# Output projection by seven block products instead of eight, in two rounds of 1024 channels

## The chip, the cores and the metric

One core of one Trainium2 chip runs the kernel. The metric is the device time of one launch in microseconds (us). The kernel before takes 2109.77 us, the median of 2 runs (2109.26 and 2110.27).

## The reference, cut to what matters

The block normalises x (2048 tokens by 1024), projects it by `w_in` to 7168 channels, and makes two branches of 1024 channels: a gated long convolution (Hyena, `y_a`) and a spatial gating unit (gMLP, `y_b`). The change touches the last two lines alone:

```python
y = jnp.concatenate([y_a, y_b], axis=-1) @ w_out      # (2048, 2048) @ (2048, 1024)
x = x + rms_norm(y, post_norm_w)
```

All of it is float32. The kernel reaches that accuracy by splitting each operand into a rounded high part and a remainder (`hi` and `lo`, type float32r) and summing three matmuls, hi·hi + lo·hi + hi·lo (`mm3`, L273 to L277).

## The kernel before, in words

**The input projection** is a stream of 56 pairs of 128-channel blocks (`stream`, L616). A pair is a 2 x 2 block product done with seven block products in place of eight (Winograd's form of Strassen's scheme). The weights are the stationary operand, in seven units of 128 x 512 that are read from DRAM, combined (`comb`, L545) and split (`prep_unit`, L556). The tokens are the moving operand, seven tiles `x0` to `x6` that stay in SBUF for 28 pairs; for the second half of the tokens they are summed early, kept in DRAM (`XS`) and read back by `load_x` (L509), which splits them again. One product is 4 k-steps of 3 matmuls of 512 columns, so a pair is 7 x 12 = 84 matmuls. Products 5 and 6 of a pair come after product 0 of the next one. The classes `TakeU`, `TakeG`, `TakeB`, `TakeV` add the partial sums from PSUM and pass them on.

**Stages.** Beside the stream, `tick` (every second step of the stream) advances background jobs and starts new ones at a given rate. The stages in their order, each with its own SBUF pool: filter MLP and its transform (`k1_jobs`); `x_jobs`, which make `XS`; `kfft_jobs`, ending with the switch to the second half of the tokens; pool `fb`, the **u stage**: pairs U(1), whose `u_job` and `u1_job` convolve, gate, transpose and transform u; pool `fc`: pairs G, V and B with `fft_jobs` and the inverse transform; then the output projection. In pool `fb` there are 4 tiles of 128 x 1024 (tag `wide`: `r1`, `rv`, `t1`, `t2` of a pair) and 3 of 128 x 512 (tag `f`: `uh`, `ul`).

**The output projection.** During the last pair, `load_wo` (L1046) reads `w_out` (8 MB) in 16 pieces through `wide` tiles, splits them, and keeps all of it in the place of `x0` to `x6`. `first_out` (L1092) does token blocks 0 and 1 at once, `out_phase` (L1100) the other 14: for a block, 2 halves x 16 channel blocks x 3 = 96 matmuls of 512 columns; then square and sum (L1144), times `post_norm_w` (L1149), reciprocal root, scale and residual (L1153), store (L1154). For 16 blocks that is 1536 matmuls.

**Order.** The order on each engine and queue is made by a planner when the program is built. It goes by estimated times: when an engine is free it issues, of the instructions that are ready by the plan, the one that stands first in the program; a tile gets its buffer at that moment. On the chip every engine and DMA queue then keeps that order and waits by semaphore. Most DMAs are issued by SyncE (SP).

Of the kernel before, what the change touches and what calls it, by code (L numbers as in the profile page):

```python
# [215 lines left out]

class Body:
# [77 lines left out]
    def build(self):  # L295
        with ExitStack() as st:
# [12 lines left out]
            self.Y = dram("Y", [NJ, 128, 16, 128])  # L309
            self.RB = dram("RB", [D])  # L310
# [4 lines left out]
            self.yq = {}  # L315
# [5 lines left out]
            self.order = B(0) + U(0) + GV(0) + U(1) + GV(1) + B(1)  # L321
# [4 lines left out]
            with self.pool("rp") as self.rp:  # L326
# [33 lines left out]
            with self.pool("op") as op:  # L360
                self.out_phase(op)
# [147 lines left out]
    def load_x(self, u):  # L509
# [3 lines left out]
        nc.sync.dma_start(t[:, 1].bitcast(F32), self.XS[u])  # L513
# [15 lines left out]
    def prep_begin(self, n):  # L529
# [5 lines left out]
        again = (kind, c) in self.seen  # L535
        self.seen.add((kind, c))
        w = [self.i["w_in"][b].rearrange("p (h k) c -> p h (k c)", h=2) for b in (b1, b2)]
# [18 lines left out]
    def prep_unit(self, rec):  # L556
# [17 lines left out]
        if u in SPILL and not again:  # L574
# [12 lines left out]
    def product(self, x, w, u, ps, first=True, last=True):  # L587
        po = ps.rearrange("q (i t) -> q i t", i=4)
        for k in range(4):
            c = slice(k * 128, k * 128 + 128)  # L590
            self.mm3(po, w[u][:, 0, c], w[u][:, 1, c], x[u][:, 0, :, c], x[u][:, 1, :, c],
                     first and k == 0, k == 3, skip_group_check=True)

    def finish_pair(self, new):
# [3 lines left out]
        x, w, take, B, C, u2 = self.prev  # L598
        self.prev = None
        self.product(x, w, 5, B, first=False)  # L600
# [3 lines left out]
        self.product(x, w, 6, C, first=False)  # L604
# [4 lines left out]
    def reload(self, new, u):  # L609

        if new == "wo":
            self.load_wo(u)
        elif new is not None:
            self.load_x(u)

    def stream(self, pairs, new=None):  # L616

        for n in range(pairs):
            h, kind, c, b1, b2 = self.order[self.at]
            take = {"U": TakeU, "G": TakeG, "B": TakeB, "V": TakeV}[kind](self, h, c)  # L620
            key, _, _, w = self.next_w
            x, rec = dict(self.X), self.next_w
            change = new if n == pairs - 1 else None
            while not w:
                self.prep_unit(rec)
            B = self.bank("proj")
            self.product(x, w, 0, B)
# [5 lines left out]
            self.next_w = self.prep_begin(self.at)  # L633
# [3 lines left out]
            self.product(x, w, 1, A)  # L637
# [4 lines left out]
            self.product(x, w, 2, B, first=False)  # L642
# [5 lines left out]
            self.product(x, w, 3, C)  # L648
# [3 lines left out]
            self.product(x, w, 4, B, first=False)  # L652
# [5 lines left out]
            self.prev = (x, w, take, B, C, u2)  # L658
# [387 lines left out]
    def load_wo(self, u):  # L1046


        if u == 0:
            self.xh, self.xl = [], []  # L1050
        if u % 2 == 0:
            self.xh.append(self.xp.tile([128, 4, D], F32R, name=f"wo{u}", tag=f"x{u}"))
            if u < 6:
                return
            lo = [self.wp.tile([128, D], F32R, name="wol", tag="wu", bufs=5) for _ in range(4)]
        else:
            t = self.xp.tile([128, 4, D], F32R, name=f"wo{u}", tag=f"x{u}")
            lo = [t[:, q] for q in range(4)]
        self.xl.append(lo)
        nc, n = self.nc, u // 2  # L1060
        for q in range(4):
            c = 4 * n + q
            raw = self.wide([128, D], "wo_raw")
            nc.sync.dma_start(raw, self.i["w_out"][c * 128:(c + 1) * 128])
            nc.scalar.copy(self.xh[n][:, q], raw)
            nc.vector.tensor_tensor(lo[q], raw, self.xh[n][:, q].bitcast(F32), op=ALU.subtract)

    def out_mms(self, ps, h, r, hi, lo):

        sl = slice(h * 512, h * 512 + 512)  # L1070
        for q in range(4):
            self.mm3(ps, hi[:, q], lo[:, q], self.xh[r][:, q, sl], self.xl[r][q][:, sl], r == 0 and q == 0, r == 3 and q == 3)

    def first_tokens(self, j):

        parts = []
        for s in range(2):
            raw = self.two("yraw")
            self.nc.sync.dma_start(raw.rearrange("q s (c p) -> q (s c) p", c=4), self.Y[j, :, 8 * s:8 * s + 8])
            if j == 0 and s:  # L1080
                pair = [[self.f("yq", F32R) for _ in range(2)] for _ in range(2)]
            else:
                tag, bufs = ("wide", self.nw_) if j else ("two", self.nl)
                pair = [[t[:, 0], t[:, 1]] for t in [self.fp.tile([128, 2, 512], F32R, name="yq", tag=tag, bufs=bufs) for _ in range(2)]]
            for r in range(2):
                hi, lo = pair[0][r], pair[1][r]
                self.nc.scalar.copy(hi, raw[:, r])
                self.nc.vector.tensor_tensor(lo, raw[:, r], hi.bitcast(F32), op=ALU.subtract)
                parts.append([x.rearrange("q (c p) -> q c p", c=4) for x in (hi, lo)])
        return parts  # L1090

    def first_out(self):  # L1092
        self.banks = {}
        for j in range(2):
            parts = self.first_tokens(j)
            self.banks[j] = [self.bank("proj" if j == 0 else "b") for _ in range(2)]
            for h, r in [(h, r) for h in range(2) for r in range(3)] + [(0, 3), (1, 3)]:
                self.out_mms(self.banks[j][h], h, r, *parts[r])

    def out_phase(self, op):  # L1100
        nc, i = self.nc, self.i
        xv = i["x"].rearrange("(p j) d -> j p d", j=NJ)
        ov = self.out.rearrange("(p j) d -> j p d", j=NJ)
        pw = op.tile([128, D], F32, name="pw")
        nc.scalar.dma_start(pw, i["post_norm_w"].partition_broadcast(128))
        jk = op.tile([128, 512], F32, name="jk")
        z = lambda: op.tile([128, 512], F32, name="z", bufs=4)
        xt = lambda j: op.tile([128, D], F32, name=f"xt{j % 2}")
        q = lambda j: op.tile([128, 8, 128], F32R, name=f"q{j % 2}", bufs=4)
        ld = lambda: op.tile([128, 8, 128], F32, name="yraw", bufs=4)  # L1110

        first = {"z": [z()], 0: [xt(0)], 3: [q(3)], 1: [xt(1)], 2: [q(2)], "ld": [ld()]}
# [74 lines left out]
```

## Time and profile before

| | |
|---|---|
| median of 2 runs | 2109.77 us |
| the profiled execution | 2112.95 us, span 2111.2 us |
| TensorE matmul busy | 1944.8 us (92%), 8024 matmuls, mean granted clock 0.974 |
| TensorE weight load busy | 1451.6 us (69%) |
| VectorE (DVE) busy | 1217.0 us (58%) |
| ScalarE (ACT) busy | 786.5 us (37%) |
| GpSimd (POOL) busy | 378.8 us (18%) |
| DMA moved | 469.75 MB, mean 223 GB/s |

Times are microseconds from the start of the span unless marked ns. A matmul's busy time (0.39 us) is longer than its share of the engine, because matmuls are pipelined; where they follow each other without a gap, the time of a stretch divided by their number counts. An engine's idle time is put down to what released it last. The rows themselves are in the section after the change.

### The profile page before, as it was taken

The page shows a single profiled execution, that of the slowest core. Times are in us where ns is not written, and L with a number is a line of the kernel's source. Part 1 is how long each engine was busy: PE and PEld are TensorE (multiplying, and loading weights), DVE is VectorE, ACT ScalarE, POOL GpSimd, SP SyncE. Part 2 cuts the span into 40 slices and gives each one's busy share as a digit, 9 for nine tenths or more (in the row PEclk, how much of TensorE's full clock was granted, in tenths as well). Part 3 has the DMA queues.
Part 4 walks back from the last instruction along what each step waited for, and adds up shares of the span by engine and source line. Part 5 has one row for each costly group of instructions (what it writes and reads, how often), then busy time and mean ns, then how long its engine had stood idle before and what let it go on. Part 6 is the DMA issues. An engine that isn't in the chain of part 4 may idle for free.

```text
span 2111.2 us, 23743 instructions
## 1 busy us (share of the span) xinstructions
PE 1944.8 (92%) x8024; PEld 1451.6 (69%) x8024; DVE 1217.0 (58%) x1912; ACT 786.5 (37%) x1426; POOL 378.8 (18%) x342
## 2 busy tenths in 40 slices
PE   3698999998999989899999999899999996999998
PEld 3465666777776766677776566557677775788887
DVE  6768877787564645744446889778642243322221
ACT  5344444664544434444543232233222232211110
POOL 3421322223222111111111101001011100100100
PEclk9899999999999999999999999999999998999999
DMA  5388776785879778866668878797989864432311
GB/s 143 108 265 279 231 260 235 245 287 204 270 241 303 256 276 260 295 174 200 204 203 257 289 255 278 257 289 254 298 271 291 273 216 159 160 110 90 107 63 40
DMA packets 318105, 469.75 MB, mean 223 GB/s; under 512 B 106363, under 2 KB 176251, under 8 KB 317055
## 3 DMA queue, kind: packets, MB, share of 16 engines
q1 hardware_dynamic: 251232, 393.44, 57.5%
q10 hardware_dynamic: 61856, 69.81, 9.8%
q0 software_dynamic: 4896, 4.98, 1.0%
q8 instruction: 64, 1.05, 0.2%
q14 instruction: 57, 0.47, 0.1%
HBM read 286.74 MB, written 181.41 MB: 222 GB/s over the span
## 4 chain that ended last, share of the span: by engine, by line
PE 47%; DVE 7%; DMA 4%; issue 2%; ACT 1%; POOL 0%; SPq 0%; DVEq 0%; ACTq 0%; POOLq 0%
PE proj L277 11%; PE proj L276 11%; PE proj L275 11%; PE b L1035 3%; PE b L1009 2%; PE b L997 2%; DVE pb L1000 1%; DMA wo_raw<-in_w_out_dram 1%; PE b L275 1%; DVE pa L1000 1%; PE b L276 1%; PE b L277 1%; PE b L924 1%; DVE t L807 1%; DVE pa L1004 1%
## 5 line engine op out<-in xcount | busy, mean ns | idle before, releaser
L275 PE MATMUL proj<-x,wu 128*128 128x512 f32 x1568 | 658.0, 420 | 24.6 <-ACT x L461 13.1
L276 PE MATMUL proj<-x,wu 128*128 128x512 f32 x1568 | 632.9, 404 | 8.7 <-DVE wu L570 6.9
L277 PE MATMUL proj<-x,wu 128*128 128x512 f32 x1568 | 632.1, 403 | 0.6 <-POOL x L462 0.6
L275 PEld LDWEIGHTS proj<-x,wu 128*128 128x128 f32 x1568 | 299.0, 191 | 113.5 <-issue 29.5
L570 POOL TENSOR_TENSOR wu<-wraw,wu 128x512 fp32r<-128x512 f32 x140 | 207.6, 1484 | 929.5 <-ACT wu L568 747.7
L276 PEld LDWEIGHTS proj<-x,wu 128*128 128x128 f32 x1568 | 299.0, 191 | 94.4 <-issue 25.4
L277 PEld LDWEIGHTS proj<-x,wu 128*128 128x128 f32 x1568 | 298.9, 191 | 76.0 <-issue 13.0
L568 ACT CAST wu<-wraw 128x512 fp32r<-128x512 f32 x168 | 104.0, 619 | 250.5 <-PE proj L277 214.0
L275 PE MATMUL proj<-wo,q 128*128 128x512 f32 x448 | 174.3, 389 | 0.9 <-ACT q L1122 0.9
L276 PE MATMUL proj<-wo,q 128*128 128x512 f32 x448 | 174.4, 389 | 0.5 <-DVE q L1123 0.5
L570 DVE TENSOR_TENSOR wu<-ws,wu 128x512 fp32r<-128x512 f32 x112 | 83.7, 748 | 101.4 <-ACT wu L568 101.3
L581 ACT COPY sn<-proj 128x512 f32<-128x512 f32 x168 | 97.7, 582 | 90.5 <-PE proj L277 75.2
L277 PE MATMUL proj<-wo,q 128*128 128x512 f32 x336 | 130.7, 389 | 0.0
L568 ACT CAST wu<-ws 128x512 fp32r<-128x512 f32 x112 | 69.2, 619 | 116.9 <-PE proj L277 89.8
L1000 DVE TENSOR_TENSOR pa<-b,k 64x512 f32<-64x512 f32 x128 | 87.4, 683 | 41.9 <-PE b L997 28.3
L275 PEld LDWEIGHTS proj<-wo,q 128*128 128x128 f32 x448 | 84.0, 188 | 18.7 <-ACT q L1122 1.3
L276 PEld LDWEIGHTS proj<-wo,q 128*128 128x128 f32 x448 | 84.1, 188 | 18.5 <-DVE q L1123 1.0
L1123 POOL TENSOR_TENSOR q<-yraw,q 128x1024 fp32r<-128x1024 f32 x14 | 33.5, 2394 | 315.4 <-ACT q L1122 315.4
L1000 DVE TENSOR_TENSOR pb<-b,k 64x512 f32<-64x512 f32 x128 | 88.8, 694 | 1.8
L1009 PE MATMUL b<-pa,tb 128*128 128x512 f32 x128 | 71.9, 647 | 14.0 <-DVE pa L1004 5.6
L1148 DVE TENSOR_TENSOR ss<-ss 128x1 f32<-128x1 f32 x16 | 23.1, 1443 | 88.0 <-ACT jk L1144 88.0
L1011 ACT COPY ev<-b 128x512 f32<-128x512 f32 x64 | 37.4, 586 | 96.9 <-PE b L1009 95.7
(200 smaller groups left out, 2740.4 us busy)
## 6 DMA issues: line engine op xcount, KB each, us to landing
wraw<-in_w_in_dram SPq DMA_DIRECT2D x84, 512.0 KB, 5.2
WSB<-wu SPq DMA_DIRECT2D x32, 512.0 KB, 4.7
dd<-in_c_dec_dram SPq DMA_DIRECT2D x32, 512.0 KB, 5.9
AK<-ev ACTq DMA_DIRECT2D x64, 256.0 KB, 3.8
WSU<-wu SPq DMA_DIRECT2D x32, 512.0 KB, 4.2
WSG<-wu SPq DMA_DIRECT2D x32, 512.0 KB, 5.0
raw<-AK SPq DMA_DIRECT2D x32, 512.0 KB, 6.1
KF<-ev ACTq DMA_DIRECT2D x32, 512.0 KB, 5.7
```

Of the source, the lines that this page charges most:

```text
L275: t.matmul(ps, sh, mh, start=first, stop=False, **kw)
L276: t.matmul(ps, sl, mh, start=False, stop=False, **kw)
L277: t.matmul(ps, sh, ml, start=False, stop=last, **kw)
L568: nc.scalar.copy(w[:, 0], src[u])
L570: eng.tensor_tensor(w[:, 1], src[u], w[:, 0].bitcast(F32), op=ALU.subtract)
L581: self.nc.scalar.copy(s, ps)
L997: nc.tensor.matmul(u, tv[0][:, n], raw[:, n], start=True, stop=True)
L1000: nc.vector.tensor_tensor(o, uu, kk, op=ALU.mult)
L1009: nc.tensor.matmul(ps, tv[1][:, n], prod[n], start=True, stop=True)
L1011: nc.scalar.copy(ev, ps)
L1035: nc.tensor.matmul(ps, g1[:, d], raw[:, d], start=d == 0, stop=d == 1)
L1123: (nc.gpsimd if r else nc.vector).tensor_tensor(lo, raw, hi.bitcast(F32), op=ALU.subtract)
```

## The change

The stream goes on over 16 more pairs, of kind "O", in two rounds: `O(0)` takes channels 0 to 1023 of `Y` (the Hyena half), `O(1)` channels 1024 to 2047 (the gMLP half). A pair is two blocks of 128 tokens. Now the tokens are the stationary operand, read from `Y` and combined and split as the weights of a new pair are, and seven combinations of the 2 x 2 blocks of `w_out` are the moving one, in the place of `x0` to `x6`. Round 0 writes its sums to DRAM (`PT`); round 1 reads them back (`o_load`), adds, and does the norm, the residual and the store (`o_job`). The seven factors of each round lie in DRAM (`WT`, 14 MB): four of them are made by `wo_jobs` beside the u stage, from 16 reads of 512 KB, with 32 subtractions and 32 stores of 256 KB; the other three are plain blocks, copied from `w_out` to `WT` by DMAs from DRAM to DRAM, six of 1 MB in all. Before the last two products of the last B pair, `rest()` finishes the background jobs, and only then the first O pair begins. `load_wo`, `out_mms`, `first_tokens`, `first_out` and `out_phase` go. With `flat`, `product` takes a moving tile's k-step as one run of 512 columns.

```diff
+class TakeO(Take):
+    def c11(self, A, s1):
...
+    def c22(self, C, u3):
+        self.y[1] = self.b.wide([128, 1024], "y1")
+        self.b.add(self.y[1][:, 512:], C, u3)
+        if self.h:
+            self.part = [self.b.o_load(2 * self.c + 1 - n) for n in range(2)][::-1]
+
+    def c21(self, B):
+        y = self.y[1][:, :512]
+        if self.h:
+            self.nc.vector.tensor_tensor(y, B, self.part[1][:, :512], op=ALU.add)
+            self.b.go(self.b.o_job(2 * self.c + 1, self.y[1], self.part[1], 512))
+        else:
+            self.nc.scalar.copy(y, B)
+            self.nc.sync.dma_start(self.b.PT[2 * self.c + 1], self.y[1])
...
+            O = lambda r: [(r, "O", m, 2 * m, 2 * m + 1) for m in range(8)]
+            self.order = B(0) + U(0) + GV(0) + U(1) + GV(1) + B(1) + O(0) + O(1)
...
                     self.nw_, self.nf = 4, 3
...
+                    self.background(self.wo_jobs(), 0.32)
                     self.run(self.stream(8))
-                    self.drain()
+                    self.rest()
                 with self.pool("fc") as self.fp:
                     self.nw_, self.nf, self.nl = 4, 6, 4
                     self.background(self.fft_jobs(), 1.0)
-                    self.run(self.stream(20, "wo"))
-                    self.rest()
-                    self.first_out()
-            with self.pool("op") as op:
-                self.out_phase(op)
+                    self.run(self.stream(20, "w0"))
+                with self.pool("fo") as self.fp:
+                    self.nw_ = 4
...
+                    self.run(self.stream(8, "w1"))
+                    self.run(self.stream(8))
+                    self.drain()
...
+    def wo_jobs(self):
+        for r in range(2):
+            for q in range(4):
+                yield self.wo_job(r, q)
+            for u, k, c in ((0, 0, 0), (1, 1, 0), (6, 1, 1)):
+                rows = (8 * r + 4 * k) * 128
+                self.nc.sync.dma_start(self.WT[r, u], self.i["w_out"][rows:rows + 512, 512 * c:512 * c + 512].rearrange("(q p) c -> p q c", p=128))
+
+    def wo_job(self, r, q):
+        nc = self.nc
+        raw = []
+        for k in range(2):
+            raw.append(self.wide([128, 2, 512], "wo_raw"))
+            rows = (8 * r + 4 * k + q) * 128
+            nc.sync.dma_start(raw[k].rearrange("p h c -> p (h c)"), self.i["w_out"][rows:rows + 128])
+        yield
+        (b11, b12), (b21, b22) = [(t[:, 0], t[:, 1]) for t in raw]
+        t1, t2, t3, t4 = [self.f(n) for n in ("t1", "t2", "t3", "t4")]
+        for t, x, y, u in ((t1, b12, b11, 3), (t2, b22, t1, 2), (t3, b22, b12, 4), (t4, b21, t2, 5)):
+            nc.vector.tensor_tensor(t, x, y, op=ALU.subtract)
+            nc.sync.dma_start(self.WT[r, u, :, q], t)
...
             self.prev = (x, w, take, B, C, u2, flat)
+            if turn:
+                self.rest()
+                self.next_w = self.prep_begin(self.at)
+                self.prep_unit(self.next_w)
...
+    def o_job(self, j, y, part, done):
+
+        nc, fp = self.nc, self.fp
+        xr = fp.tile([128, D], F32, name="xr", bufs=3)
+        nc.sync.dma_start(xr, self.i["x"].rearrange("(p j) d -> j p d", j=NJ)[j])
+        nc.vector.tensor_tensor(y[:, done:], y[:, done:], part[:, done:], op=ALU.add)
+        ss = fp.tile([128, 1], F32, name="ss", bufs=2)
+        nc.scalar.activation(part, y, AF.Square, accum_out=ss)
+        nc.vector.tensor_tensor(y, y, self.pw, op=ALU.mult)
+        rs = self.rstd(fp, ss)
+        nc.vector.scalar_tensor_tensor(y, y, rs, xr, op0=ALU.mult, op1=ALU.add)
+        nc.sync.dma_start(self.out.rearrange("(p j) d -> j p d", j=NJ)[j], y)
```

## Rows read from the trace of the kernel before

**Rows 1.** Windows of the span: engine busy (x instructions), granted clock, DMA share, GB/s.

```profile
core 0: us, PE busy (x) PEld busy (x) DVE busy (x) ACT busy (x) POOL busy (x), PEclk, DMA share, GB/s
0.00:46.00 46.00, 19.14 (x83) 14.88 (x84) 27.00 (x40) 29.79 (x61) 12.94 (x13) 0.98 0.59 154
330.00:525.00 195.00, 181.62 (x796) 142.51 (x795) 153.69 (x177) 105.88 (x218) 59.26 (x67) 1.00 0.70 241
855.00:1085.00 230.00, 211.36 (x965) 170.19 (x963) 118.18 (x187) 107.86 (x205) 38.99 (x41) 0.97 0.69 211
1500.00:1725.00 225.00, 224.77 (x956) 166.75 (x955) 88.66 (x167) 60.57 (x102) 30.69 (x24) 1.00 0.83 269
1725.00:1799.40 74.40, 52.73 (x219) 41.56 (x217) 28.43 (x32) 23.32 (x31) 0.00 (x0) 0.86 0.49 158
1799.40:2104.80 305.40, 304.88 (x1344) 252.11 (x1344) 82.87 (x102) 51.74 (x99) 33.51 (x14) 1.00 0.29 97
```

**Rows 2.** Waits of PE from 1715 to 1800: total, times, longest.

```profile
PE proj L275 <- ACT yq L1087: 19.4, 1, 19.4
PE proj L275 <- ACT q L1122: 0.9, 1, 0.9
```

**Rows 3.** Windows inside the turn to the output projection.

```profile
1744.00:1763.40 19.40, 0.01 (x1) 0.00 (x1) 10.17 (x10) 9.03 (x10) 0.00 (x0) 0.58 0.88 278
1763.40:1799.40 36.00, 35.09 (x145) 28.29 (x145) 5.25 (x10) 5.92 (x13) 0.00 (x0) 0.94 0.21 71
```

**Rows 4.** End of the timeline: start, duration, what.

```profile
2104.72 0.39 PE L277 MATMUL proj<-wol,q 128*128 128x512 f32 x1
2105.20 0.60 ACT L1144 ACTIVATE jk<-proj 128x512 f32<-128x512 f32 x1 [10.19 <-PE proj L277]
2107.57 0.99 SPq L1154 DMA_DIRECT2D out_dram<-z  x2
```

**Rows 5.** Groups by line and form: count | busy us, mean ns | idle before.

```profile
L570 DVE TENSOR_TENSOR wu<-ws,wu 128x512 fp32r<-128x512 f32 x112 | 83.7, 748 | 101.4 <-ACT wu L568 101.3
L547 DVE TENSOR_TENSOR ws<-wraw 128x512 f32<-128x512 f32 x28 | 24.0, 856 | 42.3 <-DMA wraw<-in_w_in_dram 42.2
L585 DVE TENSOR_TENSOR r<-proj,sn 128x512 f32<-128x512 f32 x64 | 43.8, 685 | 34.0 <-PE proj L277 31.8 <-PE b L277 1.8
L771 DVE TENSOR_TENSOR l<-l,dd 128x1024 f32<-128x1024 f32 x32 | 42.4, 1326 | 13.3 <-ACT dd L770 13.3
L410 DVE SCALAR_TENSOR_TENSOR xt<-xt,rs,pw 128x1024 f32<-128x1024 f32 x16 | 24.5, 1529 | 0.7 <-DVE rs L525 0.3
L518 DVE TENSOR_TENSOR x<-x 128x1024 fp32r<-128x1024 f32 x14 | 17.5, 1294 | 8.7 <-ACT x L517 8.7
L408 ACT ACTIVATE jk<-xt 128x1024 f32<-128x1024 f32 x16 | 17.0, 1065 | 9.3 <-DMA xt<-in_x_dram 8.7 <-ACT sn L581 0.6
L570 POOL TENSOR_TENSOR wu<-wraw,wu 128x512 fp32r<-128x512 f32 x140 | 207.6, 1484 | 929.5 <-ACT wu L568 747.7 <-DMA BY<-ev 34.2 <-DMA wu<-WSU 25.7
L547 POOL TENSOR_TENSOR ws<-wraw 128x512 f32<-128x512 f32 x28 | 49.4, 1763 | 127.6 <-DVE wu L570 75.2 <-DMA wraw<-in_w_in_dram 22.4 <-issue 11.3
L547 POOL TENSOR_TENSOR ws<-wraw,ws 128x512 f32<-128x512 f32 x28 | 38.0, 1355 | 138.5 <-DVE wu L570 130.0 <-DVE rs L525 8.5
```

**Rows 6.** Timeline from 16 to 19, DVE and POOL.

```profile
16.45 0.69 DVE L547 TENSOR_TENSOR ws<-wraw 128x512 f32<-128x512 f32 x1 [1.03 <-DMA wraw<-in_w_in_dram]
17.18 1.63 DVE L547 TENSOR_TENSOR ws<-ws,wraw 128x512 f32<-128x512 f32 x1
16.57 1.69 POOL L547 TENSOR_TENSOR ws<-wraw 128x512 f32<-128x512 f32 x1 [14.62 <-DMA wraw<-in_w_in_dram]
```

**Rows 7.** DMA issues: count, KB each, median us from issue to landing.

```profile
wo_raw<-in_w_out_dram SPq DMA_DIRECT2D x16, 512.0 KB, 4.6
x<-XS SPq DMA_DIRECT2D x7, 1024.0 KB, 7.7
XS<-t SPq DMA_DIRECT2D x16, 256.0 KB, 3.3
```

**Rows 8.** The tile g: duration ns min/median/max, first and last start.

```profile
L1035 PE MATMUL b<-raw,g x128: 590/592/1061, 1365.4 to 1707.9; 128*128 128x512 f32 x128
L1019 SPq DMA_DIRECT2D g<-in_c_g_dram x1: 340/340/340, 368.7 to 368.7; - x1
```

**Rows 9.** Timeline of SP's DMA queue near the start.

```profile
19.27 0.43 SPq L539 DMA_DIRECT2D wraw<-in_w_in_dram  x1
25.08 1.11 SPq L401 DMA_DIRECT2D xt<-in_x_dram  x2
```

More of the change, by code (lines that the diff above doesn't have):

```diff
@@ L214, in c12 @@
             self.b.go(self.b.v_job(self.h, self.c + n, vr))
+class TakeO(Take):
+    def c11(self, A, s1):
+        self.y = [None, None]
+        self.y[0] = self.b.wide([128, 1024], "y0")
+        self.b.add(self.y[0][:, :512], A, s1)
+    def c22(self, C, u3):
[11 more added lines that the diff above has]
+            self.nc.sync.dma_start(self.b.PT[2 * self.c + 1], self.y[1])
+    def c12(self, C, u2):
+        self.b.add(self.y[0][:, 512:], C, u2)
+        if self.h:
+            self.b.go(self.b.o_job(2 * self.c, self.y[0], self.part[0], 0))
+        else:
+            self.nc.sync.dma_start(self.b.PT[2 * self.c], self.y[0])
 class Body:
@@ L573, in prep_unit @@
         self.to_spill = []
-        if u in SPILL and not again:
+        if u in SPILL and not again and key[0] != "O":
             self.to_spill = [(self.WS[key][SPILL.index(u)], w.bitcast(F32))]
@@ L585, in add, with product @@
         self.nc.vector.tensor_tensor(out, view(ps), view(sn), op=ALU.add)
-    def product(self, x, w, u, ps, first=True, last=True):
-        po = ps.rearrange("q (i t) -> q i t", i=4)
+    def product(self, x, w, u, ps, flat, first=True, last=True):
+        po = ps if flat else ps.rearrange("q (i t) -> q i t", i=4)
         for k in range(4):
             c = slice(k * 128, k * 128 + 128)
-            self.mm3(po, w[u][:, 0, c], w[u][:, 1, c], x[u][:, 0, :, c], x[u][:, 1, :, c],
-                     first and k == 0, k == 3, skip_group_check=True)
+            hi, lo = [x[u][:, r, k] if flat else x[u][:, r, :, c] for r in range(2)]
+            self.mm3(po, w[u][:, 0, c], w[u][:, 1, c], hi, lo, first and k == 0, k == 3, skip_group_check=True)
     def finish_pair(self, new):
@@ L597, in finish_pair @@
             return
-        x, w, take, B, C, u2 = self.prev
+        x, w, take, B, C, u2, flat = self.prev
         self.prev = None
-        self.product(x, w, 5, B, first=False)
+        self.product(x, w, 5, B, flat, first=False)
         take.c21(B)
@@ L603, in finish_pair @@
         yield
-        self.product(x, w, 6, C, first=False)
+        self.product(x, w, 6, C, flat, first=False)
         take.c12(C, u2)
@@ L609, in reload @@
     def reload(self, new, u):
[L611 to L614, printed above, removed]
+        if new is not None:
+            self.load_x(new, u)
     def stream(self, pairs, new=None):
@@ L632, in stream @@
             self.at += 1
-            self.next_w = self.prep_begin(self.at)
+            turn = change == "w0"
+            self.next_w = None if turn else self.prep_begin(self.at)
             yield
@@ L641, in stream @@
             yield
-            self.product(x, w, 2, B, first=False)
+            self.product(x, w, 2, B, flat, first=False)
             u2 = self.snap(B, "s2")
@@ L651, in stream @@
             yield
-            self.product(x, w, 4, B, first=False)
+            self.product(x, w, 4, B, flat, first=False)
             u3 = self.snap(B, "s1")
@@ L1043, in inv_job @@
         nc.sync.dma_start(self.Y[j, :, 4 * h:4 * h + 4], xg.rearrange("q (c p) -> q c p", c=4))
[L1046 to L1090, printed above, removed]
```

97 lines of the change are left out of this document (27 added, 70 removed).

## The prediction, made before the change was run

> **What bounds the kernel now.** I read the windows of the span first, then the waits of TensorE (PE) at the turn to the output projection, then the end of the timeline, then the groups of instructions that the new pairs will use. In the windows [rows 1] the reader is to see that PE sets the time: from 1799.4 to 2104.8 it is busy for 304.88 of 305.40 us with 1344 matmuls, so one matmul of 512 columns takes 305.4 / 1344 = 0.2272 us and nothing else matters there. The window before it, 1725.0 to 1799.4, is loose: 192 matmuls of token blocks 0 and 1 and two products (24) of the last B pair should take 216 x 0.2272 = 49 us, and it lasts 74.4. One wait of 19.4 us makes most of that [rows 2]: PE stands until token block 1 has been split, which comes behind the 16 pieces of `w_out`. PE does nothing then, the granted clock is 0.58 in that stretch and 0.94 over the 36 us after it [rows 3], so some matmuls after it run at the lower of its two levels, 1.2 GHz. The whole output part, 1725.0 to 2104.8, is 379.8 us for 1560 matmuls, and 1560 x 0.2272 = 354.4: 25.4 us are lost.
>
> **What the change takes away.** Eight block products become seven: 16 pairs x 84 = 1344 matmuls in place of 1536, 192 x 0.2272 = 43.6 us. `load_wo` and `first_out` go, and with them the 25.4 us. With PE packed, the output part would be (1344 + 24) x 0.2272 = 310.8 us: **69.0 us less**. The rest is what comes back.
>
> **The tail, +5.** Now the last matmul starts at 2104.72 and the span ends at 2111.2, 6.5 us later, with the work in halves of 512 [rows 4]. `o_job` works on 1024 elements after `c12`: add of the last half 0.69, add of `part` 1.33, square 1.07, root and reciprocal about 0.7 with waits, scale and residual 1.53 [rows 5], a store of 512 KB in place of 256. That is 5.3 us before the store and about 4 for it, and DVE still has up to 2 us of block 2c + 1 when product 6 ends: 9.5 to 12 us. It can't come out below zero, since every step is at least as long as before; range 3 to 6.
>
> **Round 0, nothing.** A pair has 84 x 0.2272 = 19.1 us of PE. DVE does five splits (5 x 0.748), two combinations (2 x 0.856) and three adds from PSUM (3 x 0.685) [rows 5]: 7.5 us, 39%. The window 1500 to 1725 has DVE at 88.66 / 225 = 39% as well, and PE idles 0.2 us in it [rows 1]. If that cover goes, it is round 1.
>
> **Round 1, +9.** To these come one more add from PSUM (0.685), the adds of `part` (0.69 and 1.33), two products with `pw` (2 x 1.326) and two scalings (2 x 1.529) [rows 5]: 15.9 of 19.1 us, 83%. The nearest stretch is 330 to 525, DVE at 153.69 / 195 = 79%, and there PE idles 13.4 us, 6.9% [rows 1]. 6.9% of 8 x 19.1 is 10.5; I take 9, as part of that idle time is the stage's end. Lower end 0. The upper end is what follows if DVE and POOL can't work at once: POOL has two splits (2 x 1.484) and two combinations (1.763 + 1.355), 6.1 us a pair [rows 5]; 15.9 + 6.1 = 22.0 against 19.1, so 8 x 2.9 = 23 us. What DVE is late for is the splits of the next pair's units, and behind them product 1 or 2.
>
> The Trainium skill speaks against the change here: its page "SBUF — State Buffer", section "Who interferes with whom", says that a DVE instruction with both inputs in SBUF contends with a GpSimd instruction that reads SBUF, because they share a read port. The trace agrees: the same DVE subtraction takes 0.69 us alone and 1.63 with POOL's beside it [rows 6]. By the rows alone the round gives back 9; by the page's rule taken fully it would be the 23 above.
>
> **The two switches of the moving tiles, +4, and the first O pair, +1.5.** A factor of 1 MB lands in 7.7 us [rows 7], then come a cast (about 1.07) and a subtraction (1.294) for each half [rows 5]: 11.4 us. The tile is needed six products, 16.3 us, after it came free, so one load is covered. But seven loads and a pair's own 2 MB are 9.4 MB in 19.1 us, and the window 1500 to 1725 moves 269 GB/s at a share of 0.83, 324 GB/s at full share [rows 1]: 29 us, 10 too many, 5 of them covered. So 0 to 5 us at each switch, 2 taken. The first O pair loads two blocks of 512 KB (4.6 us for such a load [rows 7]), casts and splits: 6 us against the 5.4 of products 5 and 6 that cover it; 0 to 8, and the planner may load earlier, so 1.5.
>
> **The u stage, +6.** Eight `wo_job`s add 32 subtractions (24 us) to DVE's 118 of 230 us [rows 1, 5], and 16 reads and 32 stores, 16.8 MB, to 48.5 MB at a share of 0.69 [rows 1]; the share becomes 0.93. PE has no more work there and waits 18.6 us already. Nothing leaves this stage, so no gain. What can be late: each job needs four `f` tiles, of which there are three, and a tile is free only when its store has landed (3.3 us [rows 7]); `uh` and `ul` need them too, and the two `wo_raw` hold two of the four `wide` tiles meanwhile, for which `r1` and `rv` queue. If each store is waited for, a job takes 4 x (0.75 + 3.3) = 16 us, and the add that waits for `r1` has some 12 us before the stream needs its result: 4 us lost, 8 times, 32 at most. The lower end is 0. By DVE's busy time alone, 18.6 x 24 / 118 = 3.8; with the fuller DMA 6.
>
> **The six copies, +5.** They wait for nothing, not for a buffer either. A load of this kind shows what the planner does with it: `g`, first used at 1365.4, was issued at 368.7, when its buffer came free [rows 8]. So the copies will go out in SP's first free time, though they stand in the u stage: between 19.27 and 25.08 [rows 9], ahead of the last loads of x. 6.3 MB at 324 GB/s are 20 us of all DMA engines. In the first 46 us PE is busy for 19 [rows 1] and waits for x; DVE has 27 us of work there, which hides part of a delay. 0 to 20, and 5 taken, since only half of the x tiles stand behind the copies.
>
> **Sum.** -69.0 + 5 + 9 + 4 + 1.5 + 6 + 5 = -38.5. The profiled execution took 2112.95 us, its span 2111.2; 2112.95 - 38.5 = 2074.5, and it lies 3.2 above the median, so **2071 us**.
>
> **Rivals.**
> - *All is hidden* (0.20): only the tail and a few us come back, 2045 to 2056. For it: PE at 224.77 of 225 us beside a full DMA [rows 1]. Against it: every stretch with DVE near 80% has idle PE.
> - *Round 1 is set by DVE and POOL together* (0.13): 23 in place of 9, 2085.
> - *The copies hold up the start* (0.10): 20 in place of 5, 2086.
> - *Buffers of the u stage* (0.05): slower than before. The raws of the next jobs are taken into `wide` tiles as soon as these are free, so that `r1` finds none and every job costs the stream its full 16 us of stores: 8 x 16 = 128 in place of 6 gives 2193; it beats the gain from 5.6 us a job on. For it: four tiles for what needs four already. Against it: the add has three products of slack, and waiting adds stand ahead of later raws.
> - That the change does not do what it says I put at nothing: the number of matmuls is fixed by the loops.
>
> **Chances and range.** The forecast has 0.52, with 2056 to 2086 as its own range. 2% of 2109.77 is 42.2 us, about what a measurement of this kernel can tell from no change, so faster means under 2067.6. The first rival lies there whole, and of the forecast two fifths (0.22): 0.42. Two rivals and the rest of the forecast lie within 2%: 0.55. The fourth rival gives slower 0.03, as a part of it stays within 2%. The range 2048 to 2096 leaves out the lower end of the first rival, the last one, and two upper ends at once.
>
> **What would show it.** PE in the output part: 1344 matmuls at 0.227 us, and no wait near 19 us at the turn. Round 1: DVE near 83% of its window, PE idle about 9 us, with splits (L570 before) as what ended the waits. The u stage: PE idle about 25 us in place of 18.6. The start: six transfers to `WT` near 20 us, and the first B pair's second product later than before by 5. Wrong I would be first of all if the copies are issued in the u stage, where loads of split weights would stand behind them, or if round 1 shows no idle PE.

## The result, and the profile after

The changed kernel takes **2081.93 us** (two runs, 2081.43 and 2082.42) against 2109.77: a ratio of 0.9868, 95% interval 0.9826 to 0.9910, 27.8 us less. The forecast was 2071, so the change gave back some ten microseconds more than the sum had. The profiled execution took 2081.43, its span is 2079.6 us, 31.6 less than the span of before.

The span can be cut at four events that both kernels have: the first load of a spilled weight of the u stage, the last transform matmul of that stage, the last transpose of the inverse transform, and the start of the last matmul. All times in us:

| stretch | before | after | difference | predicted |
|---|---|---|---|---|
| start to the u stage | 855.2 | 853.5 | -1.7 | +5 |
| u stage | 263.1 | 279.8 | **+16.7** | +6 |
| from there to the last transpose | 595.9 | 596.2 | +0.3 | 0 |
| output part, to the last matmul's start | 390.5 | 338.6 | **-51.9** | -54.5 |
| end | 6.5 | 11.5 | +5.0 | +5 |
| sum | 2111.2 | 2079.6 | -31.6 | -38.5 |

Windows of the changed kernel (engine busy and instructions, granted clock, DMA share, GB/s); the first answers to the first of [rows 1], the last four to its last two:

```profile
0.00:46.00 46.00, 20.60 (x87) 16.12 (x88) 27.55 (x40) 29.84 (x61) 13.57 (x14) 0.99 0.94 290
1729.50:1772.70 43.20, 39.85 (x167) 31.58 (x165) 32.82 (x35) 24.51 (x34) 13.90 (x7) 0.96 0.80 285
1772.70:1925.00 152.30, 150.63 (x663) 124.44 (x664) 77.36 (x97) 62.77 (x101) 45.74 (x32) 1.00 0.49 174
1800.00:1900.00 100.00, 100.00 (x442) 82.83 (x442) 37.53 (x52) 35.01 (x60) 28.34 (x21) 1.00 0.41 142
1925.00:2068.30 143.30, 135.65 (x591) 109.89 (x589) 108.25 (x134) 59.82 (x114) 40.28 (x26) 1.00 0.57 187
```

With 0.2272 us a matmul, each stretch tells what it lost. The turn: 43.2 - 167 x 0.2272 = 5.3. Round 0 and the switch after it: 152.3 - 663 x 0.2272 = 1.7; in its middle (1800 to 1900) PE is busy for 100 of 100 us. Round 1: 143.3 - 591 x 0.2272 = 9.0, with DVE at 108.25 / 143.3 = 76%.

The wait of 19.4 us at the turn [rows 2] is gone. The chain of waits there (start, duration, what) shows what is left of it:

```profile
1737.43 7.79 DMA x<-WT
1745.24 1.06 ACT x L558
...
1750.94 1.36 DVE x L559
...
1753.18 0.69 DVE sg L652
...
1754.43 0.57 ACT sn L648
1755.05 0.50 PE proj L304
```

A factor lands in 7.79 us, ScalarE casts it and DVE subtracts, and the add that frees a bank comes behind these subtractions: PE stands for 2.6 us, and the mean granted clock of the turn's window is 0.96.

Round 1's waits of PE, 1925 to 2080 (total, times, longest), and a group of the same window:

```profile
PE proj L304 <- ACT sn L648: 5.8, 6, 1.0
PE proj L305 <- DVE wu L637: 1.9, 1, 1.9
```
```profile
L1131 ACT ACTIVATE part<-y 128x1024 f32<-128x1024 f32 x16 | 17.0, 1062 | 27.7 <-DVE y L1129 22.7 <-DVE y L232 4.8
```

Most of what PE waits for are ScalarE's snapshots of a bank, not DVE's splits. ScalarE stands for 27.7 us ahead of its squares, at the head of its own queue, because DVE's adds are late; a snapshot behind such a square is late with it. This is read from the order of the rows; no run took it away.

The end (timeline of DVE: start, duration, what; the last matmul starts at 2068.1), which answers to [rows 4]:

```profile
2068.93 0.67 DVE L652 TENSOR_TENSOR y<-proj,sn 128x512 f32<-128x512 f32 x1
2069.52 1.27 DVE L1134 SCALAR_TENSOR_TENSOR y<-y,rs,xr 128x1024 f32<-128x1024 f32 x1
2070.72 1.22 DVE L1129 TENSOR_TENSOR y<-y,part 128x1024 f32<-128x1024 f32 x1
2073.15 1.22 DVE L1132 TENSOR_TENSOR y<-y,pw 128x1024 f32<-128x1024 f32 x1 [1.21 <-ACT part L1131]
2074.48 1.28 DVE L1134 SCALAR_TENSOR_TENSOR y<-y,rs,xr 128x1024 f32<-128x1024 f32 x1
```

The scaling at 2069.52 belongs to the pair's other block. The wait of 1.21 us is for ScalarE's square: the product is written over `y`, which the square is still reading. The product then takes 1.22 us itself.

The six copies, from the timeline of SP's queue:

```profile
19.31 0.64 SPq L568 DMA_DIRECT2D WT<-in_w_out_dram  x1
...
25.63 4.42 SPq L568 DMA_DIRECT2D WT<-in_w_out_dram  x4
...
35.98 0.55 SPq L568 DMA_DIRECT2D WT<-in_w_out_dram  x1
```

They are issued where the prediction put them, and the DMA share of the first 46 us goes from 0.59 to 0.94, but PE does more there, not less (20.60 us in place of 19.14).

Last the u stage. The longest wait of PE, then two of DVE, 848 to 1118, and the landing times of two transfers of the stage from the DMA view of 850 to 1120 (count, KB, median us):

```profile
PE a L924 <- DVE ut L914: 16.5, 6, 5.3
```
```profile
DVE t L581 <- DMA wo_raw<-in_w_out_dram: 13.3, 4, 7.9
DVE t L581 <- DMA WT<-t: 9.6, 7, 2.3
```
```profile
AU<-ev ACTq DMA_DIRECT2D x56, 256.0 KB, 4.8
ut<-U SPq DMA_DIRECT2D x16, 256.0 KB, 5.1
```

DVE stands for 9.6 us because a tile `t` still waits for its store, and for 13.3 because the raw blocks have not landed; PE waits for the products `ut` behind it. The stores are waited for directly too: in the same stage `ul` waits 4.7 us and `uh` 3.4 us for a tile whose store has not landed.

### The profile page after: what moved, and what is told of

Its sections match the earlier page's. It is cut to its first block, busy times and chain, and to the rows that moved or that the text cites. A ratio compares the mean times of both kernels' runs of the same rounds, so it can differ in the third digit from the quotient of the medians.

```text
span 2079.6 us, 23943 instructions
## 1 busy us (share of the span) xinstructions
PE 1907.2 (92%) x7832; PEld 1419.1 (68%) x7832; DVE 1347.8 (65%) x2070; ACT 855.0 (41%) x1538; POOL 446.3 (21%) x392
## 5 line engine op out<-in xcount | busy, mean ns | idle before, releaser
L304 PE MATMUL proj<-x,wu 128*128 128x512 f32 x2016 | 834.9, 415 | 36.0 <-ACT sn L648 15.1
L305 PE MATMUL proj<-x,wu 128*128 128x512 f32 x2016 | 808.2, 401 | 10.6 <-DVE wu L637 8.8
L306 PE MATMUL proj<-x,wu 128*128 128x512 f32 x2016 | 806.6, 400 | 1.2 <-DVE x L559 0.6
L304 PEld LDWEIGHTS proj<-x,wu 128*128 128x128 f32 x2016 | 383.6, 190 | 146.2 <-issue 32.8
L637 POOL TENSOR_TENSOR wu<-wraw,wu 128x512 fp32r<-128x512 f32 x172 | 257.3, 1497 | 1038.1 <-ACT wu L635 855.5
L305 PEld LDWEIGHTS proj<-x,wu 128*128 128x128 f32 x2016 | 383.7, 190 | 113.3 <-issue 24.9
L306 PEld LDWEIGHTS proj<-x,wu 128*128 128x128 f32 x2016 | 383.2, 190 | 94.6 <-issue 12.7
L637 DVE TENSOR_TENSOR wu<-ws,wu 128x512 fp32r<-128x512 f32 x176 | 129.7, 739 | 156.0 <-ACT wu L635 155.6
L614 POOL TENSOR_TENSOR ws<-wraw 128x512 f32<-128x512 f32 x44 | 79.0, 1795 | 174.5 <-DVE wu L637 111.7
L614 POOL TENSOR_TENSOR ws<-wraw,ws 128x512 f32<-128x512 f32 x44 | 59.5, 1353 | 223.4 <-DVE wu L637 210.1
L559 DVE TENSOR_TENSOR x<-x 128x1024 fp32r<-128x1024 f32 x42 | 56.3, 1381 | 19.2 <-ACT x L558 19.2
L1033 PE MATMUL b<-raw,tk 128*128 128x512 f32 x128 | 62.9, 612 | 5.5 <-issue 4.8
L862 PE MATMUL b<-s,ff 128*128 128x512 f32 x128 | 62.2, 603 | 4.4 <-ACT ev L864 2.9
L1070 PE MATMUL b<-raw,tu 128*128 128x512 f32 x128 | 63.2, 604 | 1.7 <-DMA raw<-AU 1.7
```

Of the source, the lines that this page charges most:

```text
L304: t.matmul(ps, sh, mh, start=first, stop=False, **kw)
L305: t.matmul(ps, sl, mh, start=False, stop=False, **kw)
L306: t.matmul(ps, sh, ml, start=False, stop=last, **kw)
L614: eng.tensor_tensor(t, x, y, op=op)
L637: eng.tensor_tensor(w[:, 1], src[u], w[:, 0].bitcast(F32), op=ALU.subtract)
L1033: nc.tensor.matmul(ps, tv[:, n], raw[:, n], start=True, stop=True)
```

## The experiments

The open question was the u stage: 16.7 us in place of 6. The theories carry letters in the expectations. **A**: the jobs hold something that the stage's own work then waits for, either VectorE's queue, in which a subtraction that waits stops what is behind it (A1), or tiles that come free only when a store has landed (A2). **B**: the 32 subtractions' busy time on DVE. **C**: the transfers themselves, which slow the stage's other transfers. **D**: the four `wide` tiles. Every kernel is the changed one with the edit shown, and "the stage" is the u stage by the two events above. Without jobs' transfers in it the stage was 261.2, 261.5, 262.1 and 263.1 us in four kernels; with the jobs unchanged it was 279.8 and 283.8 in two, so differences under 4 us say nothing.

**No jobs.**

```
-    self.background(self.wo_jobs(), 0.32)
+    self.wo_jobs()
-        return self.WT[int(new[1]), u]
+        return self.WT[int(new[1]), (0, 1, 6)[u % 3]]
```

> The u stage makes no factors: no reads, subtractions or stores there; the output rounds read the three plain blocks of w_out in place of all seven factors, so the output is another one. The u stage is measured from the first load of a split weight of U(1) to the last f matmul: 263.1 us before the change, 279.8 after. If the stage's loss is the factor work, whatever part of it, the stage is 263 +- 2 and the time 2065 +- 3. If the loss came from elsewhere (the longer rest, the copies at the start), it stays near 280 and 2082.

The factor jobs are taken out of `wo_jobs` itself too, so that only its six copies are issued. The stage was 261.2 us and the kernel 2056.95 (before on the same chip 2108.47). So the jobs cost the stage all of its growth, and the six copies, which stayed in, cost nothing that shows. The longest wait of PE from 848 to 1118, and the same two transfers as above:

```profile
PE a L922 <- DVE ut L912: 9.9, 8, 2.7
```
```profile
AU<-ev ACTq DMA_DIRECT2D x64, 256.0 KB, 2.8
ut<-U SPq DMA_DIRECT2D x16, 256.0 KB, 2.9
```

Both transfers land in about 3 us here and in about 5 beside the jobs. The window of the stage itself shows how PE loses the time (the changed kernel, then this one):

```profile
853.50:1133.40 279.90, 248.52 (x1111) 199.10 (x1111) 154.71 (x234) 125.20 (x235) 42.97 (x44) 0.96 0.81 255
```
```profile
848.80:1110.10 261.30, 242.79 (x1114) 194.90 (x1114) 130.12 (x203) 125.00 (x235) 43.93 (x44) 0.98 0.69 210
```

The stage is 18.6 us longer with the jobs. PE idles 31.4 us in it with them and 18.5 without: 12.9 more. The other 5.7 us are in its busy time, 248.52 against 242.79 us for nearly the same instructions (1111 and 1114), at a mean granted clock of 0.96 against 0.98: part of a wait is paid a second time, by what runs at the lower level after it.

**The transfers without the subtractions.**

```
-        t1, t2, t3, t4 = [self.f(n) for n in ("t1", "t2", "t3", "t4")]
-        for t, x, y, u in ((t1, b12, b11, 3), (t2, b22, t1, 2), (t3, b22, b12, 4), (t4, b21, t2, 5)):
-            nc.vector.tensor_tensor(t, x, y, op=ALU.subtract)
+        for t, u in ((b12, 3), (b22, 2), (b11, 4), (b21, 5)):
             nc.sync.dma_start(self.WT[r, u, :, q], t)
```

> Same reads and same stores of factors, but no subtraction and no f tile: halves of the raw tiles are stored as they are, so the factors are plain blocks. Theory A (VectorE's queue stands at a subtraction that waits for a store or a load to land, and the u chain stands behind it): 263 to 266 us for the stage, time 2066 to 2069. Theory B (VectorE's added busy time alone): 263 to 265. Theory C (fuller DMA makes the loads of U0 and of split weights late): near 280, time 2082. Theory D (the raws hold wide tiles that r1, rv, t1, t2 need): 270 or more, since the raws are now held until the stores land.

284.0 us, 2087.58: the cost is all there without DVE and without a tile `f`. But now a `wide` tile is held until two stores have landed, and ScalarE's convolution waits for it:

```profile
ACT t L877 <- DMA WT<-wo_raw: 14.1, 5, 4.3
```

So this run has a new hold in place of the old one, and does not tell A2 from C.

**The subtractions without the transfers.**

```
-            raw.append(self.wide([128, 2, 512], "wo_raw"))
...
-        for t, x, y, u in ((t1, b12, b11, 3), (t2, b22, t1, 2), (t3, b22, b12, 4), (t4, b21, t2, 5)):
+        for t, x, y in ((t1, z, z), (t2, z, t1), (t3, z, z), (t4, z, t2)):
-            nc.sync.dma_start(self.WT[r, u, :, q], t)
```

> The 32 subtractions stay, on a constant tile, with their four f tiles, but nothing is read or stored, so no landing is waited for; the output rounds read the three plain blocks. Theory A: 264 to 268 us for the stage, time 2067 to 2071. Theory B: near 280, time 2082. Theories C and D: 263, 2066.

261.5 us, 2061.26. DVE's 32 subtractions and their tiles cost 0.3 us when no tile waits for a store. **B is out.**

**Five tiles f in place of three.**

```
-                    self.nw_, self.nf = 4, 3
+                    self.nw_, self.nf = 4, 5
```

> Five f tiles in the u stage in place of three. Theory A: the waits of the subtractions for a store (9.6 us in 7 waits in the trace) go, and the stage falls to about 270 to 273 us, time 2072 to 2075; the waits for the reads (13.3 us in 4) stay. Theories B, C and D: 279 to 280 and 2081 to 2082.

269.9 us, 2067.99: 9.9 us of the stage come back, what theory A expected; the time is 4 us below its estimate. DVE's waits and the two transfers, as above:

```profile
DVE t L581 <- DMA wo_raw<-in_w_out_dram: 13.3, 4, 8.6
...
DVE ul L928 <- DMA WT<-t: 0.9, 2, 0.6
```
```profile
AU<-ev ACTq DMA_DIRECT2D x60, 256.0 KB, 5.6
ut<-U SPq DMA_DIRECT2D x16, 256.0 KB, 7.0
```

The waits of a `t` for a store are gone, and only the raw loads are waited for. The stage's own transfers land no sooner (5.6 and 7.0 us). So the tiles held were half of the cost, and something else is left: 269.9 - 261.2 = 8.7 us. Whether a held tile costs by the subtraction that stops VectorE's queue (A1) or by `uh` and `ul` that find none (A2), this run does not tell: it takes away both.

**Five wide tiles.**

```
-                    self.nw_, self.nf = 4, 3
+                    self.nw_, self.nf = 5, 3
```

> Five wide tiles in the u stage in place of four, f tiles still three. The stage was 279.8 us after the change, 261.5 with subtractions but no traffic, 284.0 with the traffic and no subtractions, 269.9 with five f tiles. Theory D (the raws hold wide tiles that r1, rv, t1, t2 then wait for): 270 to 274 us for the stage and 2072 to 2077 in all. Theory C (fuller DMA makes other loads late): no change, 279 to 280 and 2081 to 2083.

283.1 us, 2083.97: no gain. The raw loads are waited for less (8.0 in place of 13.3), and the stores take over:

```profile
DVE t L581 <- DMA WT<-t: 10.2, 7, 2.6
DVE t L581 <- DMA wo_raw<-in_w_out_dram: 8.0, 2, 7.4
```

With three `f` tiles the raws are not what limits, so D falls.

**The subtractions on GpSimd.**

```
-            nc.vector.tensor_tensor(t, x, y, op=ALU.subtract)
+            nc.gpsimd.tensor_tensor(t, x, y, op=ALU.subtract)
```

> The 32 subtractions go to GpSimd; f and wide tiles stay at three and four. If the loss is that VectorE's queue stands at a subtraction (theory A1), the u chain on VectorE is free of it and the stage falls to 263 to 270 us, time 2066 to 2073. If it is that uh, ul, r1 and the others find no buffer (theory A2, D), who subtracts does not matter, and as GpSimd takes about twice as long the buffers are held longer: 278 to 285, time 2081 to 2087.

287.2 us, 2086.93. DVE's queue no longer holds a subtraction that waits for a store, and the stage is not shorter. DVE waits for the tiles themselves:

```profile
DVE ul L928 <- DMA WT<-t: 9.1, 1, 9.1
DVE r L652 <- POOL t L581: 8.2, 2, 7.0
```

`ul`, the split's lower part, needs a tile `f` whose store is on its way for 9.1 us: A2 is seen here without A1. But A1 is not refuted for the changed kernel, since this run has a new hold. GpSimd's queue, which also makes splits for PE, now stands 52.6 us at the subtractions for their raw blocks, and VectorE 8.2 us for GpSimd.

**Half of the jobs in another stage.** Round 0's four jobs stay, with five tiles; round 1's four run beside the first output pairs.

```
-                    self.nw_, self.nf = 4, 3
-                    self.background(self.wo_jobs(), 0.32)
+                    self.nw_, self.nf = 4, 5
+                    self.background(self.wo_jobs(0), 0.16)
...
+                    self.background(self.wo_jobs(1), 0.25)
```

> A version meant to be better: only round 0's four jobs in the u stage, with five f tiles; round 1's four beside O(0), with raws in part's tiles and three f tiles of their own. The u stage should be 264 to 268 us (half of the 8.4 us that are left with five f tiles), and O(0), where VectorE is at half load, should stay packed: 2062 to 2067. If the buffers of O(0) are as short as those of the u stage, the loss only moves there and it is 2068 to 2074.

268.1 us; 2070.25 (four runs, 2065.03 to 2075.42, before 2111.1), a ratio of 0.9804 (0.9773 to 0.9834). The output part stayed at 338.3 us, so four jobs cost nothing beside round 0; the time lies in the rival's range, but the loss did not move there. The profiled execution, 2072.82, came to the u stage 5.9 us later than the changed kernel did. But half of the traffic left the u stage 5.0 to 6.9 us longer than none (263.1, 261.2), where all of it with five tiles cost 8.7 to 13.0 over 261.2 (the runs at 269.9 and 274.2): the two can't be told apart within the spread.

**The product with the norm's weight on GpSimd.**

```
-        nc.vector.tensor_tensor(y, y, self.pw, op=ALU.mult)
+        nc.gpsimd.tensor_tensor(y, y, self.pw, op=ALU.mult)
```

> The product with post_norm_w in round 1 goes from VectorE to GpSimd, the rest as after the change. Round 1 (143.3 us from 1925.0 to 2068.3 in the trace after, 9.0 above 591 matmuls at 0.2272) has VectorE at 76%. If VectorE's load makes those 9 us, they fall to about 4 and the tail stays or grows by 1 us: 2077 to 2079. If GpSimd's product takes VectorE's time through a shared port, or the wait is ScalarE's square in front of the snapshots, no gain: 2081 to 2084.

2095.74, a miss of both estimates; the output part grew from 338.6 to 354.7 us and the end from 11.5 to 13.2 (the u stage was 283.8 us, 4 longer, with nothing changed in it). DVE got rid of 1.29 us a block, and yet its busy time in round 1 did not fall: 109.43 us here, where the changed kernel's window from 1925.0 has 108.25. Round 1 in this run, then groups of the window 1925 to 2080, first the changed kernel, then this one:

```profile
1922.00:2080.80 158.80, 143.35 (x591) 115.39 (x589) 109.43 (x120) 59.95 (x114) 78.08 (x41) 0.95 0.51 169
```
```profile
L1134 DVE SCALAR_TENSOR_TENSOR y<-y,rs,xr 128x1024 f32<-128x1024 f32 x16 | 26.8, 1675 | 0.1
L637 DVE TENSOR_TENSOR wu<-wraw,wu 128x512 fp32r<-128x512 f32 x6 | 4.0, 674 | 0.0
L652 DVE TENSOR_TENSOR y<-proj,sn 128x512 f32<-128x512 f32 x22 | 14.9, 677 | 3.5 <-ACT sn L648 3.5
```
```profile
L1132 POOL TENSOR_TENSOR y<-y,pw 128x1024 f32<-128x1024 f32 x14 | 33.8, 2412 | 16.9 <-ACT part L1131 16.2
L1134 DVE SCALAR_TENSOR_TENSOR y<-y,rs,xr 128x1024 f32<-128x1024 f32 x14 | 28.6, 2040 | 3.4 <-POOL y L1132 3.0
L637 DVE TENSOR_TENSOR wu<-wraw,wu 128x512 fp32r<-128x512 f32 x6 | 14.0, 2340 | 8.6 <-ACT wu L635 8.6
L637 DVE TENSOR_TENSOR wu<-ws,wu 128x512 fp32r<-128x512 f32 x26 | 18.5, 713 | 11.2 <-ACT wu L635 11.1
L652 DVE TENSOR_TENSOR y<-proj,sn 128x512 f32<-128x512 f32 x21 | 13.9, 678 | 1.8 <-ACT sn L648 1.4 <-PE proj L306 0.3
```

Six DVE splits that read two tiles on the chip went from 674 to 2340 ns, the scaling from 1675 to 2040; the add that reads a bank of PE's results stayed at 678. The 26 splits of combined units read two tiles as well and stayed at 713 (714 in the changed kernel), so it is not the operands alone: an instruction pays when it runs beside GpSimd's, as the split at 1960.68, which took 2.46 us beside a product of GpSimd from 1960.21 to 1962.59. The rule of the Trainium skill's page "SBUF — State Buffer", section "Who interferes with whom", names just these: a DVE instruction with two inputs in SBUF contends with a GpSimd instruction that reads SBUF, one with a single input there, outside the two-port modes, does not. The trace agrees, with these three pairs of numbers. For PE, the same 591 instructions took 7.7 us more of busy time (135.65 and 143.35, at a granted clock of 1.00 and 0.95) and 7.8 us more of idle time.

**The transfers through a tile of their own.**

```
-            raw.append(self.wide([128, 2, 512], "wo_raw"))
+            raw.append(self.fp.tile([128, 2, 512], F32, name="wo_raw"))
...
-        t1, t2, t3, t4 = [self.f(n) for n in ("t1", "t2", "t3", "t4")]
...
+        for t, u in ((b12, 3), (b22, 2), (b11, 4), (b21, 5)):
             nc.sync.dma_start(self.WT[r, u, :, q], t)
```

> The changed kernel without the subtractions (their operands' raw halves are stored in place of the differences), as in e2, but the raw halves pass through one tile of their own: the sixteen loads and the thirty-two stores of the factors stay in the u stage, and no job holds a tile that a convolution or an operand's split waits for. Theory A2 (held tiles): the stage falls back to 260 to 266 us (e1 261.2), time 2056 to 2062. Theory C (the transfers themselves get in the way of the stage's other transfers): the stage stays at 278 to 285 us (e2 284.0), time 2075 to 2088. Between the two, the share of each is read off.

279.2 us, 2075.32: nothing that the stage needs is held, and the cost is there. By its expectation that is C. But its loads wait for the tile at the head of SP's queue, which is new as well:

```profile
SPq L580 <- DMA wo_raw<-in_w_out_dram: 52.6, 16, 5.1
SPq L576 <- DMA WT<-wo_raw: 47.5, 14, 4.8
```

Behind these 100 us stand the stage's own loads. So this run is not clean either.

**Five tiles f, and the product to another tile.**

```
-        nc.scalar.activation(part, y, AF.Square, accum_out=ss)
-        nc.vector.tensor_tensor(y, y, self.pw, op=ALU.mult)
+        jk = fp.tile([128, D], F32, name="jk")
+        nc.scalar.activation(jk, y, AF.Square, accum_out=ss)
+        nc.vector.tensor_tensor(part, y, self.pw, op=ALU.mult)
...
-        nc.vector.scalar_tensor_tensor(y, y, rs, xr, op0=ALU.mult, op1=ALU.add)
+        nc.vector.scalar_tensor_tensor(y, part, rs, xr, op0=ALU.mult, op1=ALU.add)
```

> Five tiles f as in e4, and in the end of an output pair the product with the norm's weight is written to the tile of the partial sums, and the square's unused output to one of its own, so that VectorE's product no longer waits for ScalarE's square. Theory: the end after the last matmul's start falls from 11.5 to 10.3 us (the 1.21 us wait is gone), round 1's waits for a snapshot stay (ScalarE's square is still ahead of the snapshot in its queue), time 2066 to 2067.5. Rival: in round 1 VectorE's idle time ahead of that product (8.6 us in sixteen pairs) holds its queue, and without it the waits for a snapshot fall from 5.8 us to under 3, time 2062 to 2065. u stage 268 to 272 us by both.

2073.22 (four runs, 2069.25 to 2074.56, before 2110.41), a ratio of 0.9823 (0.9808 to 0.9838). The end went from 11.5 to 10.1 us; DVE no longer waits there (timeline):

```profile
2064.53 1.23 DVE L1129 TENSOR_TENSOR y<-y,part 128x1024 f32<-128x1024 f32 x1
2065.79 1.23 DVE L1133 TENSOR_TENSOR part<-y,pw 128x1024 f32<-128x1024 f32 x1
```

The rival falls: PE's waits for a snapshot did not shrink (11.8 us from 1715 on; 10.2 in the changed kernel), so DVE's wait for the square was not what made them. The stage was 274.2 us, 4.3 longer than with the same five tiles before, and the output part 340.3, 2.9 longer; by these the kernel's time missed both estimates, and the 1.4 us of the end do not show in it.

**The jobs earlier.**

```
-                    self.background(self.x_jobs(1), 0.25)
+                    self.background(self.xw_jobs(), 0.6)
...
-                    self.background(self.wo_jobs(), 0.32)
```

> The eight factor jobs leave the u stage for the stage in which the second half of x is turned (from about 530 to 690 us), which has eight tiles f and four wide ones; nothing else is changed. Theory A2 (held tiles): the u stage is back at 260 to 264 us, the earlier stage grows by under 5 us, time 2057 to 2065. Theory C (the transfers themselves): the 16 MB that the jobs move cost the earlier stage 10 to 20 us, as they did the u stage, time 2070 to 2080.

`xw_jobs` gives two factor jobs after each of the four jobs of `x_jobs(1)`. 2101.68 (five runs, before 2110.41), a ratio of 0.9947: a miss of both. The u stage is back at 262.1, but it starts at 898.7 us, 45 later. I had put the earlier stage at the wrong time: the jobs' loads were issued from 381 to 530 us, in the stretch in which DVE is busiest of all [rows 1]. A window of the changed kernel, then of this one:

```profile
375.00:560.00 185.00, 173.13 (x771) 139.34 (x770) 142.15 (x159) 104.36 (x220) 58.53 (x65) 0.99 0.72 243
```
```profile
375.00:560.00 185.00, 148.23 (x613) 116.42 (x612) 133.04 (x159) 83.77 (x179) 42.27 (x50) 0.91 0.82 281
```

PE did 158 instructions less there, 36 us of work at 0.2272, with 14.1 us of waits for ScalarE's copy `rv` that were not there before, and the granted clock fell from 0.99 to 0.91. Eight tiles `f` did not help. Whether DVE's work or the tiles that the convolutions share with the raws set this was not tried.

**The same bytes from DRAM to DRAM.**

```
...
+        nc.scalar.dma_start(self.WT[r, 2:6, 0, q, 0:1], mark)
...
-            nc.sync.dma_start(raw[k].rearrange(...), self.i["w_out"][rows:rows + 128])
+            nc.sync.dma_start(self.WX[r, q].rearrange(...)[k], self.i["w_out"][rows:rows + 128])
...
-            nc.vector.tensor_tensor(t, x, y, op=ALU.subtract)
-            nc.sync.dma_start(self.WT[r, u, :, q], t)
+            nc.sync.dma_start(self.WT[r, u, :, q], self.i["w_out"][rows:rows + 128, 512 * h:512 * h + 512])
```

> The changed kernel with its factor jobs turned into copies from DRAM to DRAM, beside the u stage as before: sixteen of 512 KB from w_out to a scratch buffer in place of the loads, thirty-two of 256 KB from w_out's halves into the places of the stored factors in place of the stores (so no difference is computed), all on SP's queue. As many transfers and bytes through the DMA engines, but no tile on the chip is held and no transfer waits for VectorE or for a store to land; two tiny transfers of four words on ScalarE's queue ahead of each job keep the copies in this stage. Theory C (the transfers themselves): the stage stays at 276 to 286 us (e9 279.2, e2 284.0), time 2072 to 2088. Theory A2 with SP's queue (what the jobs hold: tiles, and the queue while a transfer waits): the stage falls to 260 to 266 us (e1 261.2), time 2053 to 2062.

271.1 us, 2073.17 (before 2106.96): between the two theories. As many bytes, with no tile held and no wait for VectorE, cost 271.1 - 261.2 = 9.9 us. ScalarE, which stores the transform's results, now waits for its earlier stores, and PE behind it (waits of ACT, then of PE, 848 to 1118):

```profile
ACT sn L652 <- DMA AU<-ev: 8.1, 2, 5.6
ACT ev L940 <- DMA AU<-ev: 7.3, 3, 4.2
```
```profile
PE b L304 <- ACT uh L932: 4.3, 4, 3.4
PE proj L304 <- ACT sn L652: 2.2, 1, 2.2
```

PE's idle time is 5.7 us above that of the run without jobs, its busy time 4.2. This run has a hold of its own as well, the tiny transfers in ScalarE's queue: it stands 5.2 us among the first of them and 2.1 behind a later one. But the two longest of PE's new waits (3.4 and 2.2) do not follow on these: the longer one comes behind 5.6 us in which ScalarE stands at its stores.

**What follows for the stage.** Two causes of about ten microseconds each. The tiles `f`, held until a store lands: 9.9 us, by three tiles against five (279.8 and 283.8 against 269.9 and 274.2, so 5.6 to 13.9 by the choice of the pair). The transfers as such: 9.9 us by the copies, and 8.7 to 13.0 by what five tiles leave over (269.9 and 274.2 against 261.2). With runs that differ by 4 us these fit the 16.7 measured, and neither makes it alone. Open are the first part's way (through VectorE's queue, A1, or straight to `uh` and `ul`, A2) and the second's (slower landings, or SP's queue behind transfers in flight).

## Why the prediction was right, and where it was not

**The output part: right.** 51.9 us less, predicted 54.5. The turn, round 0 and the switches lost 5.3 + 1.7 = 7.0 us, predicted 5.5; round 1 lost 9.0, predicted 9. The mechanism was half right: DVE is what is late, but it reaches PE through ScalarE's snapshots (5.8 us) more than through the splits that I named (1.9). The 9 was a share of idle time taken over from another stage, so that it fits to the tenth is luck.

What I read in [rows 6] does not hold as I put it: the 0.69 us were not "alone". POOL's subtraction began 0.12 us after that DVE subtraction and ran beside it too, and the two read different tiles. What shows the contention is the run with the product on GpSimd.

**The end: right** at +5.0, in part by luck. The sum left out the product, which waits 1.21 us for the square and then takes 1.22; the run with the product apart gave 1.4 back.

**The copies: right place, wrong price.** They fill the first 46 us' DMA to 0.94, and the u stage starts 1.7 us sooner, not 5 later. The twelve kernels that have the copies and are alike up to there started it between 848.0 and 859.4 us, 852.3 in the mean. So no cost shows; as the kernel before has one trace (855.2), a few microseconds are not excluded. The rival with 20 us is out.

**The u stage: right mechanism, wrong size; the step that failed.** I wrote that each job needs four tiles of three and that a tile is free only when its store has landed, bounded that by 32 us, and then took 6, scaled from DVE's busy share (3.8) with a little for the fuller DMA. The bound went by `r1`, which queues for a `wide` tile; that way does not show, as a fifth `wide` tile gave nothing (283.1). The subtractions' time is worth 0.3 us; the held tiles, which I had only as a bound, and the transfers, for which I took the 2 us from 3.8 to 6, are worth about ten each. 10.7 of the stage's 16.7 us are this step.

**The reference run.** I took 3.2 us off, because the profiled execution of before lay that far above its median. The profiled execution after lies 0.5 below its own. So of the 10.9 us by which the forecast was short, 6.9 are the sum's (31.6 in place of 38.5 in the span) and most of the rest is this.

**The rivals.** All hidden: no, the u stage and round 1 gave back 25.7 us. Round 1 set by DVE and POOL together, 23 us: no, 9; but the run with the product on GpSimd shows that such a price is real as soon as POOL's work there grows (the output part 16.1 us longer). Slower by 128 us of buffers: no; the price of the held tiles was 1.2 us a job, not 16.

A version that looks better stands beside it: five tiles `f` and the product apart, 0.9823 against the changed kernel's 0.9868; with half of the jobs moved, 0.9804. These intervals overlap one another, and the changed kernel's at their edges; the stage's lengths, 268.1 to 274.2 against 279.8 and 283.8, do not.

## What to carry to other kernels

A tile that is stored to DRAM costs its buffer for the whole landing time of the store: count the tiles that are under way, not the instructions that fill them, and when a bound of that kind is the only large one in a step, price the step from it and not from the engine's busy share. Work that is moved beside a full stage pays for its transfers too, and an experiment that takes one hold away should be looked through for the hold that takes its place. Before an operation goes to the engine that looks idle, look at which operands both engines read.

## What the runs showed of the hardware that was not expected

- Six copies of 1 MB from DRAM to DRAM, issued from 19.3 to 36.0 us, raised the DMA share of the first 46 us from 0.59 to 0.94 and what was moved from 154 to 290 GB/s, and PE was busy for longer, not for less.
- The same 256 KB transfers of the u stage landed in 2.8 and 2.9 us where the stage had a DMA share of 0.69, and in 4.8 and 5.1 where it had 0.81.
- In the stretch into which the jobs were moved too early, PE's waits grew and its granted clock fell from 0.99 to 0.91. In round 1 with the product on GpSimd, 7.8 us more of idle time went with 7.7 us more of busy time for the same 591 instructions, at a granted clock of 0.95 in place of 1.00: part of what a wait costs is in the matmuls behind it.
